# Four modulation chunks of layer 1 formed during the attention of layer 0 instead of during the dense SwiGLU

## Chip, cores and metric

One NeuronCore of a Trainium2 chip runs the whole program. The metric is the device time of one launch in microseconds (us), as the median of three runs. A further launch is recorded instruction by instruction by the hardware profiler; the rows below come from that one.

## What is computed

The reference is a trunk of two layers over 256 latent tokens and 256 context tokens of width 1024. Each layer modulates its input, mixes tokens (a gated linear recurrence, windowed attention and differential attention), and then mixes channels: a dense SwiGLU in layer 0, top-2 of 8 SwiGLU experts in layer 1. The part that matters here is the modulation of each layer:

```python
mod_l = jnp.split((silu_c @ ada_w[layer] + ada_b[layer])[:, None, :], 6, axis=-1)
mod_c = jnp.split(silu_cc @ ada_w[layer] + ada_b[layer], 6, axis=-1)
u_lat = h_lat * (1.0 + mod_l[1]) + mod_l[0]
...
h_lat = layer_norm(DEEPNORM_ALPHA * h_lat + mod_l[2] * m_lat, ln_g[layer, 0], ln_b[layer, 0])
u_lat = h_lat * (1.0 + mod_l[4]) + mod_l[3]
```

`ada_w[layer]` has 1024 rows and 6 x 1024 columns, all in f32: 24 MB a layer. The product has only two rows, one for the latent tokens and one for the context tokens. Of layer 1, the chunks 0 and 1 are wanted when layer 0 is over, chunk 2 after the token mixing of layer 1, chunks 3 and 4 ahead of its experts and chunk 5 after them.

## The kernel before

A scheduler orders each engine's instructions from the program text; tile pools with few buffers decide who waits for whom.

**A modulation group.** `ada(l, g, rowp)` forms two of a layer's six chunks and returns eight closures, called steps here. A step (`step`, L248 to L259) loads 128 rows by 2048 columns of `ada_w` (1 MB) into a tile `raw` by SP's queue and multiplies them by the two conditioning columns, with four matmuls of 512 columns. Each of the four writes two rows of the one PSUM bank `A`, at partition 0, 32, 64 or 96. All eight steps of a group add into that bank. The last step of a group also copies the four pairs of rows out (`row`, L292, two copies on ACT and two on DVE) and transposes them to columns (L295, sixteen 32x32 transposes on PE, in PSUM tiles `T`). `raw` has two buffers, and they also hold the weights of `w_in`, `w_out` and of the SwiGLU's first two products.

**Where the steps are called.** `self.todo` is a list of closures and `fill(n)` calls the next n of them. In the attention, `streams` alternates between a differential head part and a windowed head part for the four token blocks and calls `fill(1)` in every second round; what is left over is called by `fill(99)` when the rounds are done. In layer 0 the list holds the groups (0, 1) and (0, 2): 16 steps. In the dense SwiGLU, `ffn` runs over 11 slices of 256 hidden columns; a slice has 96 matmuls of the two products with W1 and W3 (PSUM tiles `acc` and `S`) and 48 of the product with W2 (PSUM tiles `T`), all 128x512 from its second slice on, and between the two calls `fill(2)`. There the list holds the groups (1, 0) and (1, 1), another 16 steps, with the `mods` of the first group between them.

**After the attention** comes `project`: it loads `w_out` into the `raw` buffers (L780, L783), splits each f32 weight into two parts (`whi` by a cast on ACT, L126; `wlo` by a subtraction on DVE, L127) and multiplies by three matmuls (L107 to L109), as all big products here do. At the end of the attention POOL's queue loads `ctx` and `x` into `hc` and `hl` (L1294, L1295), 1 MB each.

Of the kernel before, what the change touches and what calls it, by code (L numbers as in the profile page):

```python
# [76 lines left out]
class Trunk:  # L77
# [249 lines left out]
    def streams(self, a, b):  # L327

        rest, live, tails, n = [list(a), list(b)], [None, None], [], 0
        while any(live) or any(rest) or tails:  # L330
            tails = [g for g in tails if next(g, self) is not self]
            for j in range(2):
                if j == 1 and n < 6:
                    continue
                if live[j] is None and rest[j]:
                    live[j] = rest[j].pop(0)
                if live[j] and next(live[j]) == "tail":
                    tails.append(live[j])
                    live[j] = None
            n += 1  # L340
            if n % 2 == 0:
                self.fill(1)

    def fill(self, n):
# [898 lines left out]
    def run(self):  # L1243
        tc, nc, i = self.tc, self.nc, self.i
        self.banks = {"acc": 2, "S": 3, "T": 2, "A": 1}
        self.cat = consts(0)[1]
        self.todo, self.cols = [], {}
        all4, lat = [0, 1, 2, 3], [2, 3]
        with ExitStack() as es:
            pool = lambda name, bufs, **kw: es.enter_context(tc.tile_pool(name=name, bufs=bufs, **kw))  # L1250
            self.cp = pool("cp", 1)
            self.stp = pool("stp", 4)
            self.rawp = pool("rawp", 2)
            self.wp = pool("wp", 5)
            pool("edge", 1, side="right").tile([P, 24], F32, name="edge")
            mx = ExitStack()
            right = lambda name, bufs, **kw: mx.enter_context(tc.tile_pool(name=name, bufs=bufs, side="right", **kw))
            self.ps = mx.enter_context(tc.tile_pool(name="ps", bufs=8, space=PSUM))
            self.utp = right("utp", 8)
            self.bdp = right("bd", 1)  # L1260
            rw = right("rw", 1)

            with tc.tile_pool(name="adaw", bufs=6) as adaw, tc.tile_pool(name="u32", bufs=2) as u32p, tc.tile_pool(name="tmp", bufs=1) as self.tmp:
                self.setup()
                into = self.pairs("uh"), self.pairs("ul")
                x = [self.tmp.tile([P, 2, D], F32, name=name) for name in ("xc", "xl")]
                first = self.ada_first(rw, adaw)
                for h in range(2):
                    for k in range(KD):
                        next(first)  # L1270
                        if h:
                            next(products)
                    G, B = self.mods(0, 0, None, slice(4 * h, 4 * h + 4))
                    if h == 0:
                        for n, name in enumerate(("ctx", "x")):
                            nc.sync.dma_start(out=x[n], in_=i[name].rearrange("o (b p) d -> p (o b) d", p=P))
                    uh, ul = self.make_u(lambda tb: x[tb // 2][:, tb % 2], G, B, all4, u32p, into, (2 * h, 2 * h + 1))
                    if h == 0:
                        held = self.copied.ins
                        products = self.lru_products(0, uh, ul, False)  # L1280
                        next(products)
                with tc.issue_after(held):
                    self.params(self.tmp.tile([P, 2048], F32, name="scratch"))
                    bd = self.gate_weights(0)
            self.todo = self.ada(0, 1, rw) + self.ada(0, 2, rw)
            mh, ml = self.mixer(0, uh, ul, all4, bd, products)
            self.dumpm(mh, ml, 0)
            bd = self.gate_weights(1)
            hl = pool("hl", 1).tile([P, 2, D], F32, name="hl")
            with tc.tile_pool(name="hc", bufs=1) as hcp:  # L1290
                hc = hcp.tile([P, 2, D], F32, name="hc")
                h = lambda tb: hc[:, tb] if tb < 2 else hl[:, tb - 2]
                with tc.tile_pool(name="raw2", bufs=2) as raw2, tc.tile_pool(name="ga", bufs=1) as gp, tc.tile_pool(name="res", bufs=1) as self.resp:
                    nc.gpsimd.dma_start(out=hc, in_=i["ctx"].rearrange("o (b p) d -> p (o b) d", p=P))  # L1294
                    nc.gpsimd.dma_start(out=hl, in_=i["x"].rearrange("o (b p) d -> p (o b) d", p=P))  # L1295
                    gate = self.gate(0, 2, [0, 1], gp)
                    G, B = self.mods(0, 3, (0, 0))
                    self.project(0, mh, ml, all4, gate, h, lambda tb: self.norm(h(tb)), raw2)
                self.dumph("ln0", h, all4)
                with tc.tile_pool(name="acc", bufs=1) as accp, tc.tile_pool(name="raw2", bufs=1) as raw2, tc.tile_pool(name="wp2", bufs=3) as wp2, \  # L1300
                        tc.tile_pool(name="fg", bufs=4) as fg:
                    with tc.tile_pool(name="u32", bufs=2) as u32p:
                        uh, ul = self.make_u(h, G, B, [2, 3, 0, 1], u32p)
                    with tc.tile_pool(name="lg", bufs=1) as lgp:
                        self.base(0, 0, h, all4, lgp)
                    with tc.tile_pool(name="ga", bufs=1) as gp, tc.tile_pool(name="res", bufs=1) as self.resp:
                        m1 = []
                        self.todo = self.ada(1, 0, rw) + [lambda: m1.extend(self.mods(1, 0, (0, 1)))]
                        self.todo += self.ada(1, 1, rw)
                        self.ffn(uh, ul, h, (accp, raw2, wp2, fg), lambda: self.gate(0, 5, [0, 1], gp), lambda s: self.fill(2))  # L1310
                        self.fill(99)

                self.dumph("ln1", h, all4)
                G, B = m1
                with tc.tile_pool(name="u32", bufs=2) as u32p:
                    uh, ul = self.make_u(h, G, B, all4, u32p)
            m2 = {}

            def prepare():
                g1 = right("g1", 1)  # L1320
                self.todo.append(lambda: m2.update(gate=self.gate(1, 2, [0], g1)))
                self.todo.append(lambda: m2.update(cols=self.mods(1, 3, (1, 0))))
                self.todo.append(lambda: m2.update(G=self.rows(m2["cols"][0][:, 0], g1, "modg")))
                self.todo.append(lambda: m2.update(B=self.rows(m2["cols"][1][:, 0], g1, "modb")))

            self.todo = self.ada(1, 2, rw)
            h = lambda tb: hl[:, tb - 2]
            with tc.tile_pool(name="lg", bufs=1) as lgp:
                self.base(0, 1, h, lat, lgp)
            self.moe_consts(pool("rc", 1))  # L1330
            mh, ml = self.mixer(1, uh, ul, lat, bd, self.lru_products(1, uh, ul, True), prepare)
            self.dumpm(mh, ml, 1)
            self.RB, self.wn = 7, 0
            self.rawb = pool("rawb", self.RB)
            ro = pool("ro", 1)
            gate2 = self.gate(1, 5, [0], ro)[0]
            with ExitStack() as ms:
                rs = ExitStack()
                rp = rs.enter_context(tc.tile_pool(name="rp", bufs=1))
                u = rp.tile([P, 2, D], F32, name="u")  # L1340
                with tc.tile_pool(name="res", bufs=1) as self.resp:
                    self.project(1, mh, ml, lat, m2["gate"], h, lambda tb: self.modulate(h(tb), u[:, tb - 2], m2["G"], m2["B"]))
                    first = [self.wtile(v) for v in self.up_views(NE - 1, *self.CHUNKS[0])]
                self.dumph("ln2", h, lat)
                mx.close()
                self.ps = pool("psm", 8, space=PSUM)
                self.banks = {"h": 4, "T": 2, "Y": 2}
                pl = lambda name, bufs, side: ms.enter_context(tc.tile_pool(name=name, bufs=bufs, side=side))
                fin = self.moe(hl, u, gate2, ro, rs, pl, first)
                self.final(hl, fin)  # L1350
# [41 lines left out]
```

## Time and profile before

| what | value |
|---|---|
| median of 3 runs | 1671.74 us (1671.57 to 1671.98) |
| the profiled execution | 1673.18 us, its span 1671.3 us |
| PE (TensorE matmul) | 1587.6 us busy, 95% |
| DVE, ACT, POOL | 1221.2, 919.8, 160.9 us busy |
| attention of layer 0 | 156.8 to 268.1 us of the span |
| dense SwiGLU | some 320 to 720 us |
| DMA | 364.77 MB, 218 GB/s on average |

PE is the engine that is busy nearly all the time. The profile models the ends of matmuls, so its share says that it is seldom left without work, not that it does as much as it could.

### The profile page before, as it was taken

Reading aid. Unit: us, or ns where it says so; the run is one execution under the profiler, and the core shown is the slowest. Engines: PE = TensorE matmul, PEld = TensorE weight load, DVE = VectorE, ACT = ScalarE, POOL = GpSimd, SP = SyncE. Lnnn points to the kernel's source line nnn. Section 1 sums busy time; section 2 is a strip of 40 time slices with the busy share of each in tenths; the row PEclk is TensorE's granted clock in tenths of the full one; section 3 lists DMA queues with packets and bytes.
Section 4 is the critical chain, followed back from the end, with each engine's and each line's share of the span. In section 5 each row is a group of like instructions: output and inputs, shape, how many; then the busy total and the mean of one; then the engine's idle time right before and its main releaser. Section 6 shows DMA issues by size and latency. Waiting matters only on the chain. (4 is left out here: it accounts for less than half of the span.)

```text
span 1671.3 us, 21565 instructions
## 1 busy us (share of the span) xinstructions
PE 1587.6 (95%) x7977; PEld 1229.7 (74%) x7977; DVE 1221.2 (73%) x1741; ACT 919.8 (55%) x1298; POOL 160.9 (10%) x131
## 2 busy tenths in 40 slices
PE   7999999999999999989899799999999999999995
PEld 3776566787777777777567588787887878878784
DVE  2678675644443345687976998989888898888987
ACT  2466565423222223246665487777776776767773
POOL 0000012250000000260002200101001010010101
PEclk8999999999999999989999799999999999999998
DMA  8313446224542354212348599898998989989890
GB/s 304 121 54 104 152 152 201 101 94 158 170 157 101 126 166 162 76 54 82 113 141 285 177 393 358 322 377 304 352 347 312 344 316 341 356 310 335 325 355 31
DMA packets 164582, 364.77 MB, mean 218 GB/s; under 512 B 8396, under 2 KB 46120, under 8 KB 159352
## 3 DMA queue, kind: packets, MB, share of 16 engines
q1 hardware_dynamic: 159472, 355.56, 60.6%
q0 software_dynamic: 1840, 6.67, 1.2%
q10 hardware_dynamic: 3160, 1.12, 0.3%
q8 instruction: 64, 1.05, 0.3%
q14 instruction: 46, 0.38, 0.1%
HBM read 362.27 MB, written 1.05 MB: 217 GB/s over the span
## 5 line engine op out<-in xcount | busy, mean ns | idle before, releaser
L127 DVE TENSOR_TENSOR wlo<-rawb,whi 128x1024 fp32r<-128x1024 f32 x362 | 436.0, 1249 | 34.5 <-ACT whi L126 30.6
L126 ACT CAST whi<-rawb 128x1024 fp32r<-128x1024 f32 x362 | 364.3, 1051 | 57.0 <-PE ps_h L109 33.6
L127 DVE TENSOR_TENSOR wlo<-raw,whi 128x1024 fp32r<-128x1024 f32 x214 | 269.2, 1279 | 100.1 <-ACT whi L126 98.7
L126 ACT CAST whi<-raw 128x1024 fp32r<-128x1024 f32 x214 | 218.7, 1051 | 183.8 <-DMA raw<-in_ffn_w_dram 85.6
L108 PE MATMUL ps_h<-wlo,th 128*128 128x512 f32 (+1 forms) x672 | 257.6, 383 | 14.2 <-DVE wlo L127 13.3
L107 PE MATMUL ps_h<-whi,th 128*128 128x512 f32 (+1 forms) x672 | 253.7, 378 | 0.2 <-ACT th L131 0.2
L109 PE MATMUL ps_h<-whi,tl 128*128 128x512 f32 (+1 forms) x672 | 251.8, 375 | 0.0
L108 PEld LDWEIGHTS ps_h<-wlo,th 128*128 128x128 f32 x672 | 127.3, 189 | 51.2 <-DVE wlo L127 30.6
L107 PEld LDWEIGHTS ps_h<-whi,th 128*128 128x128 f32 x672 | 127.5, 190 | 23.0 <-ACT th L131 0.5
L109 PEld LDWEIGHTS ps_h<-whi,tl 128*128 128x128 f32 x672 | 127.4, 190 | 20.6 <-DVE tl L132 0.2
L108 PE MATMUL ps_Y<-wlo,gTh 128*128 128x512 f32 x308 | 122.4, 397 | 0.4
L109 PE MATMUL ps_Y<-whi,gTl 128*128 128x512 f32 x308 | 120.2, 390 | 0.0
L1132 POOL TENSOR_TENSOR hl<-hl,sct 128x512 f32<-128x512 f32 x26 | 45.0, 1759 | 679.5 <-DVE sct L1131 559.5
L107 PE MATMUL ps_Y<-whi,gTh 128*128 128x512 f32 x308 | 108.4, 390 | 0.0
L107 PE MATMUL ps_acc<-uh,whi 128*128 128x512 f32 (+1 forms) x256 | 92.4, 367 | 2.6 <-ACT whi L126 2.3
L108 PE MATMUL ps_acc<-ul,whi 128*128 128x512 f32 (+1 forms) x256 | 94.1, 368 | 0.1
L109 PE MATMUL ps_acc<-uh,wlo 128*128 128x512 f32 (+1 forms) x256 | 92.1, 361 | 0.0
L108 PE MATMUL ps_S<-ul,whi 128*128 128x512 f32 (+1 forms) x240 | 85.7, 357 | 0.0
L107 PE MATMUL ps_S<-uh,whi 128*128 128x512 f32 (+1 forms) x240 | 85.6, 357 | 0.0
L109 PE MATMUL ps_S<-uh,wlo 128*128 128x512 f32 (+1 forms) x240 | 84.9, 355 | 0.0
L107 PE MATMUL ps_acc<-whi,uh 128*128 128x512 f32 (+1 forms) x176 | 71.0, 403 | 0.0
L108 PE MATMUL ps_acc<-wlo,uh 128*128 128x512 f32 (+1 forms) x176 | 69.1, 392 | 0.2 <-DVE wlo L127 0.2
(352 smaller groups left out, 2830.3 us busy)
## 6 DMA issues: line engine op xcount, KB each, us to landing
rawb<-in_moe_w_dram SPq DMA_DIRECT2D x181, 1024.0 KB, 6.7
raw<-in_moe_w_dram SPq DMA_DIRECT2D x50, 1024.0 KB, 6.5
raw<-in_ada_w_dram SPq DMA_DIRECT2D x40, 1024.0 KB, 4.9
raw<-in_ffn_w_dram SPq DMA_DIRECT2D x33, 1024.0 KB, 7.2
raw<-in_w_in_dram SPq DMA_DIRECT2D x16, 1024.0 KB, 5.6
aw<-in_ada_w_dram SPq DMA_DIRECT2D x16, 512.0 KB, 7.0
raw<-in_w_out_dram SPq DMA_DIRECT2D x16, 512.0 KB, 5.6
lg<-in_ln_g_dram POOLq DMA_DIRECT2D x4, 512.0 KB, 4.0
```

The costliest lines, as they stand in the source:

```text
L107: mm(out, lhsT=ah, rhs=bh, start=start, stop=False)
L108: mm(out, lhsT=ah, rhs=bl, start=False, stop=False)
L109: mm(out, lhsT=al, rhs=bh, start=False, stop=stop)
L126: nc.scalar.copy(out=hi, in_=v)
L127: self.last = nc.vector.tensor_tensor(out=lo, in0=v, in1=hi, op=ALU.subtract)
L1132: (nc.vector if quick and nn else nc.gpsimd).tensor_tensor(out=hl[:, b, cs], in0=hl[:, b, cs], in1=t, op=ALU.add)
```

## The change

`streams` calls `fill(1)` after every `self.every` rounds. For layer 0 that number is 1, and its list is extended by the groups (1, 0) and (1, 1) to 32 steps; for layer 1 it is 2 as before. The list of the dense SwiGLU keeps only the `mods` closure. Only four places differ:

```diff
-            if n % 2 == 0:
+            if n % self.every == 0:
                 self.fill(1)
...
-            self.todo = self.ada(0, 1, rw) + self.ada(0, 2, rw)
+            self.todo, self.every = sum((self.ada(l, g, rw) for l, g in ((0, 1), (0, 2), (1, 0), (1, 1))), []), 1
...
-                        self.todo = self.ada(1, 0, rw) + [lambda: m1.extend(self.mods(1, 0, (0, 1)))]
-                        self.todo += self.ada(1, 1, rw)
+                        self.todo = [lambda: m1.extend(self.mods(1, 0, (0, 1)))]
...
-            self.todo = self.ada(1, 2, rw)
+            self.todo, self.every = self.ada(1, 2, rw), 2
```

What the scheduler makes of it shows in the order of PE's instructions. Early in the attention of layer 0, in the program before (`ps_A` is the bank of a modulation group, L255 the matmuls of a step, L656 and L598 to L602 scores, L568 transposes of softmax weights, L673 and L621 products with the values):

```order
L255 MATMUL ps_A<-raw,sc 2x512
L673 MATMUL ps_acc<-pT,dV 64x128 x4
L568 MATMUL ps_T<-cst,p 128x128 x4
L255 MATMUL ps_A<-raw,sc 2x512 x3
L656 MATMUL ps_S<-kdT,qT 128x512
L598 MATMUL ps_S<-kT,qT 128x512
L599 MATMUL ps_S<-kT,qT 128x512
L602 MATMUL ps_S<-maskr,eyer 128x128
L656 MATMUL ps_S<-kdT,qT 128x512
L255 MATMUL ps_A<-raw,sc 2x512
```

At the same place in the changed program:

```order
L255 MATMUL ps_A<-raw,sc 2x512 x4
L673 MATMUL ps_acc<-pT,dV 64x128 x4
L568 MATMUL ps_T<-cst,p 128x128 x4
L656 MATMUL ps_S<-kdT,qT 128x512
L598 MATMUL ps_S<-kT,qT 128x512
L599 MATMUL ps_S<-kT,qT 128x512
L602 MATMUL ps_S<-maskr,eyer 128x128
L255 MATMUL ps_A<-raw,sc 2x512 x4
```

Before, the four matmuls of a step mostly stand as one and three with other work between them; now most steps stand whole. Up to the product with `w_out`, the 16 steps of before stand in 29 pieces on PE, and the 32 steps of now in 38 pieces, the last of which holds three steps.

At the end of the attention of layer 0 on PE, before (L636 and L701 are transposes of results; L107 is the first product with `w_out`):

```order
L255 MATMUL ps_A<-raw,sc 2x512 x3
L568 MATMUL ps_T<-cst,p 128x128 x2
L621 MATMUL ps_acc<-pT,V 64x128
L701 MATMUL ps_T<-cst,mix_647 128x128 x2
L621 MATMUL ps_acc<-pT,V 64x128 x3
L568 MATMUL ps_T<-cst,p 128x128 x4
L621 MATMUL ps_acc<-pT,V 64x128
L568 MATMUL ps_T<-cst,p 128x128
L621 MATMUL ps_acc<-pT,V 64x128 x3
L568 MATMUL ps_T<-cst,p 128x128 x3
L107 MATMUL ps_acc<-whi,mh 128x512
```

And in the changed program (L295 are the transposes that end a group):

```order
L255 MATMUL ps_A<-raw,sc 2x512 x4
L568 MATMUL ps_T<-cst,p 128x128 x4
L621 MATMUL ps_acc<-pT,V 64x128 x4
L568 MATMUL ps_T<-cst,p 128x128 x2
L255 MATMUL ps_A<-raw,sc 2x512 x4
L568 MATMUL ps_T<-cst,p 128x128 x2
L621 MATMUL ps_acc<-pT,V 64x128
L636 MATMUL ps_T<-cst,ra 128x128 x4
L621 MATMUL ps_acc<-pT,V 64x128 x3
L255 MATMUL ps_A<-raw,sc 2x512 x12
L295 MATMUL ps_T<-cst,row 128x32 x12
L107 MATMUL ps_acc<-whi,mh 128x512 x2
```

Of the five last steps two stand between pieces of the attention, and the other three stand one behind the other, after all attention work and ahead of the first product with `w_out`.

SP's queue, which issues the loads, from the steps to the first slices of the SwiGLU. First before:

```order
L253 DMA raw<-in_ada_w_dram 128x2048 x16
L780 DMA raw<-in_w_out_dram 128x2x512 x2
L783 DMA raw<-in_w_out_dram 64x4x512 x2
L780 DMA raw<-in_w_out_dram 128x2x512 x2
L783 DMA raw<-in_w_out_dram 64x4x512 x2
L116 DMA raw<-in_ffn_w_dram 128x8x256 x3
```

Then in the changed program:

```order
L253 DMA raw<-in_ada_w_dram 128x2048 x32
L780 DMA raw<-in_w_out_dram 128x2x512 x2
L783 DMA raw<-in_w_out_dram 64x4x512 x2
L780 DMA raw<-in_w_out_dram 128x2x512 x2
L783 DMA raw<-in_w_out_dram 64x4x512 x2
L116 DMA raw<-in_ffn_w_dram 128x8x256 x3
```

The load of a `w_out` tile stands behind 32 step loads instead of 16, in the same two buffers.

## Rows read from the trace of the kernel before

**Rows 1.** The page: busy time of each engine over the span

```profile
PE 1587.6 (95%) x7977; PEld 1229.7 (74%) x7977; DVE 1221.2 (73%) x1741; ACT 919.8 (55%) x1298; POOL 160.9 (10%) x131
```

**Rows 2.** Windows: attention of layer 0, eight SwiGLU slices, the experts

```profile
core 0: us, PE busy (x) PEld busy (x) DVE busy (x) ACT busy (x) POOL busy (x), PEclk, DMA share, GB/s
156.80:268.10 111.30, 109.01 (x730) 62.22 (x728) 74.80 (x216) 70.13 (x198) 9.95 (x13) 1.00 0.46 152
...
371.20:676.30 305.10, 302.27 (x1401) 234.75 (x1401) 136.62 (x183) 79.64 (x95) 0.53 (x1) 1.00 0.44 145
...
940.00:1671.00 731.00, 699.40 (x3266) 568.33 (x3266) 649.33 (x650) 517.96 (x582) 47.02 (x28) 0.99 0.89 321
```

**Rows 3.** Groups on PE, 371.2 to 676.3 us: busy, mean ns, idle before, releasers

```profile
L107 PE MATMUL ps_T<-whi,gh 128*128 128x512 f32 x144 | 57.8, 401 | 0.9 <-DVE acc L901 0.4
...
L255 PE MATMUL ps_A<-raw,sc 128*2 128x512 f32 x128 | 15.4, 592 | 0.0
L295 PE MATMUL ps_T<-cst,row 32*128 32x32 f32 x32 | 3.4, 225 | 2.0 <-DVE row L292 1.1 <-ACT row L292 0.9
L307 PE MATMUL ps_T<-cst,adac 128*128 128x128 f32 x16 | 2.3, 277 | 0.0
```

**Rows 4.** Windows of PE alone: one slice, and a stretch without steps

```profile
515.78:549.07 33.29, 33.18 (x149) 1.00 0.27 95
664.27:692.65 28.38, 28.38 (x126) 1.00 0.25 82
```

**Rows 5.** Groups on PE, 156.8 to 268.1 us, the attention of layer 0

```profile
L255 PE MATMUL ps_A<-raw,sc 128*2 128x512 f32 x128 | 29.8, 592 | 0.2 <-DMA raw<-in_ada_w_dram 0.2
...
L295 PE MATMUL ps_T<-cst,row 32*128 32x32 f32 x16 | 1.3, 227 | 0.0
```

**Rows 6.** Timeline of PE, attention of layer 0: start us, us, instruction

```profile
157.38 1.04 PE L255 MATMUL ps_A<-raw,sc 128*2 128x512 f32 x8
158.35 0.50 PE L656 MATMUL ps_S<-kdT,qT 128*128 128x512 f32 x1
158.79 1.02 PE L255 MATMUL ps_A<-raw,sc 128*2 128x512 f32 x2
159.74 0.44 PE L530 MATMUL ps_T<-cst,st 128*128 128x128 f32 x2
...
245.94 0.63 PE L568 MATMUL ps_T<-cst,p 128*128 128x128 f32 x4 [0.33 <-DVE p L669]
...
263.77 0.43 PE L621 MATMUL ps_acc<-pT,V 128*64 128x128 f32 x2 [0.56 <-DVE pT L572]
...
265.89 0.50 PE L107 MATMUL ps_acc<-whi,mh 128*128 128x512 f32 x1 [0.36 <-ACT whi L126]
```

**Rows 7.** DMA issues, 157 to 260 us: count, KB each, median us to landing

```profile
raw<-in_ada_w_dram SPq DMA_DIRECT2D x14, 1024.0 KB, 4.9
raw<-in_w_out_dram SPq DMA_DIRECT2D x2, 512.0 KB, 4.3
```

**Rows 8.** DMA issues, 250 to 300 us, the start of the projection

```profile
hc<-in_ctx_dram POOLq DMA_DIRECT2D x1, 1024.0 KB, 10.3
hl<-in_x_dram POOLq DMA_DIRECT2D x1, 1024.0 KB, 14.5
```

**Rows 9.** Timeline of POOL, the issue of those two loads

```profile
268.35 0.92 POOL L1294 DMA_DIRECT2D hc<-in_ctx_dram  x1 [9.16 <-PE ps_T L636]
```

**Rows 10.** Windows ahead of the SwiGLU: PE's busy time and its granted clock

```profile
316.00:318.00 2.00, 0.65 (x4) 0.40 (x4) 1.50 (x2) 1.74 (x3) 1.26 (x1) 1.00 1.04 366
318.00:320.00 2.00, 0.35 (x3) 0.12 (x2) 2.00 (x5) 0.14 (x1) 0.00 (x0) 0.90 1.06 392
320.00:322.00 2.00, 2.00 (x8) 1.52 (x9) 1.74 (x5) 2.00 (x3) 0.55 (x1) 0.50 1.04 380
...
326.00:328.00 2.00, 2.00 (x17) 2.00 (x16) 2.00 (x4) 1.77 (x4) 0.00 (x0) 0.89 0.00 0
```

**Rows 11.** The page: issues of the expert weights, whole span

```profile
rawb<-in_moe_w_dram SPq DMA_DIRECT2D x181, 1024.0 KB, 6.7
```

## The prediction

> **What bounds the kernel now.** I read the page first: PE is busy 95% of the span [rows 1], so the question is whether a step that moves costs PE more or less where it goes. Next come the windows of the two stages. In the attention of layer 0 PE is busy 109.0 of 111.3 us, and in the stretch of the dense SwiGLU from the first to the last step 302.3 of 305.1 us [rows 2]; both run at the full granted clock (1.00, the 2.4 GHz level). Neither stage has idle time in which a step could be had for nothing: the attention's many small matmuls fill PE as fully as the SwiGLU's large ones. DMA is no bound in either (share 0.46 and 0.44) [rows 2]. So the change moves work from one full stage to another, and the sum is one of PE time at both ends, plus what the transfers add.
>
> The groups of PE then show the surprise. The 16 steps (128 records; an f32 matmul leaves two) take 15.4 us in the SwiGLU [rows 3] and 29.8 us in the attention [rows 5]. The timeline says why: a whole step (x8, four matmuls) lets the next instruction start 0.97 us later, and a single matmul of a step (x2) holds PE for 0.95 us just the same [rows 6]. The four write to four groups of columns and run side by side; a piece costs about 0.96 us whether it holds one of them or four. Before, the attention's 16 steps stand in 29 pieces, which makes 29 x 0.96 = 28 us.
>
> **What the SwiGLU gets back.** The stretch of 305.1 us holds 1401 PE instructions [rows 2], of which 128, 32 and 16 are steps, row transposes and gate transposes [rows 3]; the other 1225 are 128x512 matmuls. Without steps these ran at 0.227 us each (28.38 us for the 125 that the window holds whole), and in the slice that holds only one step, which lies ahead of the window, at 0.231 us (33.29 us for 144) [rows 4]; the difference is T banks that DVE has not yet emptied (0.4 us in all is named for the first of each three) [rows 3]. So 1225 matmuls take 278.1 to 283.0 us, the gate transposes stay (2.3), and 19.8 to 24.7 us come free. Counted directly the steps' 15.4, the transposes' 3.4 and the 2.0 us that PE waits for the row copies make 20.8 [rows 3]. With no step between, the product with W2 follows the other products at once and DVE has the time of two steps (1.9 us) less for its silu work first, so I don't take the upper end: **22.5 us less**.
>
> **What the attention pays.**
> Pieces: 38 instead of 29, the last of which holds three steps, so 40 against 29. 11 x 0.96 = **10.6 us more** (11.3 by the 1.03 us of a record). The doubling of the steps costs only a third more, since most now stand whole.
> Transposes: 32 more at a group's end. 16 take 1.3 us here [rows 5], 32 take 3.4 in the SwiGLU [rows 3]: **3.0** (2.6 to 3.4).
> Row copies: at the end of a group PE waits for ACT and DVE if its transposes stand right behind the last step. That happened once in the SwiGLU and cost 2.0 us [rows 3]; in the attention of before other work stood between and no such wait is named [rows 5]. In the new order two of four ends have nothing between, the first group's and the last one's: 0 to 4.0, taken as **3.0**, the last in full and half of the first.
> The last three steps: they stand together behind all attention work. A load is issued when the step before the last has freed its buffer, and lands 4.9 us later [rows 7]. Attention work takes (109.0 - 29.8) / (730 - 128) = 0.13 us a record [rows 2, 5], so the 14 records between the 28th and 29th step, and the 14 between the 29th and 30th, take 1.8 us each. Count from the end of the 28th step: the 29th ends at 2.8; the 30th is wanted at 4.6, lands at 4.9 and ends at 5.9; the 31st, issued at 2.8, lands at 7.7 and ends at 8.7; the 32nd, issued at 5.9, lands at 10.8 and ends at 11.8. PE waits 0.3 + 1.8 + 2.1 = 4.2 us. But POOL's 2 MB of `hc` and `hl` start when the last transposes L636 of the attention are through [rows 9], which now is ahead of those three steps, and in such a stretch a transfer of 1 MB took 10.3 and 14.5 us [rows 8]. If the 32nd step's load takes 10.3, the waits make 9.6. I take **6.5**, between the ends, since a load on SP's queue landed in 4.9 and only one of the three meets both of POOL's.
> The rule that speaks against the change stands here: the Trainium skill (Trainium Kernel Development and Optimization, Key Constraints) says that transfers issued from SP, ACT and POOL run on the same 16 DMA engines and interleave. By it the 9.6 would hold and the sum be 3.1 us higher; the 10.3 and 14.5 us agree with it.
> `w_out`: its first tile is issued when the 31st step is over, lands 4.3 us later [rows 7] at 13.0, and is cast while the last group's transposes still run; the second is issued at 11.8. Behind the group's end stand 16 gate transposes and the first half of the products as cover: **0.5** (0 to 2).
> Hidden waits: the attention's end now has 0.33 + 0.56 + 0.36 = 1.2 us of waits [rows 6], which then lie ahead of the three steps whose own waits cover the lateness: **-1.2**.
> The clock: ahead of the SwiGLU PE was busy 1.0 of 4 us, the granted clock fell to 0.50 (the 1.2 GHz level) and stayed there for some 6 us, in which 3 us of work are lost [rows 10]. The waits of the last steps make a stretch like it: PE would be idle for 7.5 us ahead of the 32nd step if its load is late, and busy 1.9 of the 4 us up to 11.8 if not. Part of the slow time would pass in the copies' wait: 0 to 3.0, taken as **2.0**.
> The Trainium skill's page TensorE: Matmul & The Clock Gate (HAM oscillation) describes the same fall for kernels whose loads leave gaps between bursts of matmuls. By it the 3.0 would be paid in full and the sum be 1.0 us higher; rows 10 agree.
>
> The `mods` closure stays in the SwiGLU on DVE, which is busy 137 of 305 us there [rows 2], and costs nothing; if that cover were gone, it would be below 1 us. In the attention the copies and small additions of two more groups go to ACT (70 of 111 us) and DVE (75 of 111) [rows 2], which have room as long as PE is the slower.
>
> Sum: 10.6 + 3.0 + 3.0 + 6.5 + 0.5 - 1.2 + 2.0 = 24.4 against 22.5: **1.9 us longer**. The profiled execution took 1673.18 us, 1.44 more than the median of the runs, so 1675.1 by its own time, and 1673.6 for the median.
>
> **The rivals.**
> *The end of the attention is cheap.* The three loads land in 4.9 us, POOL's transfers start too late to meet them, and without the long wait the clock holds: 2.3 and 2.0 less, and 1.5 less for copies that find ACT and DVE idle. That is 18.6 against 22.5, 3.9 shorter: 1667.8. For it speaks that the loads of the attention landed in 4.9 [rows 7]; against it that the tail's loads are the first to meet POOL's.
> *The end of the attention is dear.* POOL's loads are ahead of the last step's: 3.1 more, the clock's full 3.0, the first group's wait in full: 5.1 more, 1678.7. It decides from the point at which the 32nd load lands later than some 8 us after its issue.
> *The loads become the bound of the whole attention.* It would last some 128 us, 4.0 for each of 32 steps. A buffer comes round every 8.0 us; 1.0 goes to the matmuls, so a load may take 7.0 before every step waits. Expert loads landed in 6.7 at a DMA share of 0.89 [rows 2, 11], and here the rate goes from 152 to some 260 GB/s (16 MB more in 128 us). At 6.7 only steps with less than 3 us between them wait, some 0.5 to 1 us for 10 to 15 of the 32: 10 more, 1683.6. Against it: 0.2 us of such wait before [rows 5].
> That the change doesn't do what it says is excluded by the order of instructions: the steps do stand in the attention.
>
> **How the numbers follow.** From 1671.74, 0.2% is 3.3 us, about what a measurement of this kernel can tell from no change. The sum as it stands has 0.45, with 1669 to 1675 as its own range; the cheap end 0.21; the dear end 0.22; the loads as the bound 0.12. So faster by over 0.2% has 0.21, within it 0.45, slower 0.34. The range of 8 in 10 goes from 1666.5, just past the cheap end, to 1681, past the dear end, and leaves the last rival out.
>
> **What would show it right or wrong.** In the changed profile the stretch of the SwiGLU that now takes 305.1 us should take some 282.6; steps in the attention should be busy some 39 us; the three last steps should wait on `raw` 4 to 10 us; and the attention with its end should be some 24 us longer. That stretch at 288 or more, steps that wait on `raw` all through the attention, or an end of attention without waits would each make the prediction wrong.

## The result and the profile after

The changed kernel takes 1685.65 us (median of four runs, 1681.75 to 1688.66) against 1671.65 us before in the same runs: 14.0 us longer, ratio 1.0076 with a 95% interval of 1.0064 to 1.0089. The forecast was 1673.6 and its range ended at 1681.0.

The profiled execution took 1688.66 us, its span 1686.9, 15.6 more than before. PE's busy time in it, from the page, which answers to [rows 1]:

```profile
PE 1589.7 (94%) x7977; PEld 1233.7 (73%) x7977; DVE 1232.0 (73%) x1741; ACT 920.7 (55%) x1298; POOL 161.6 (10%) x131
```

PE works 2 us more and the span is 15.6 us longer, so most of what came on top is time in which PE stood still or for which the busy time tells nothing. Where it lies, two windows tell: the stage "attention" from the first modulation step to the last product with `w_out`, and the stage "SwiGLU" from the first product behind that to the last product with W2. In the trace of before (columns as in [rows 2]):

```profile
157.38:314.82 157.44, 155.15 (x951) 100.45 (x951) 98.49 (x264) 85.14 (x217) 24.66 (x26) 1.00 0.45 148
320.53:718.80 398.27, 392.75 (x1877) 311.37 (x1876) 195.26 (x249) 108.54 (x134) 40.71 (x24) 0.99 0.40 133
```

and in the changed kernel's:

```profile
155.73:352.60 196.87, 181.94 (x1112) 110.45 (x1112) 105.43 (x288) 88.09 (x221) 25.19 (x27) 0.92 0.62 203
358.30:733.75 375.45, 369.97 (x1716) 306.29 (x1716) 198.90 (x225) 106.24 (x130) 41.24 (x23) 1.00 0.29 96
```

The SwiGLU gives back 22.8 us, as forecast (22.5). The attention pays 39.4 instead of 24.4, and its mean granted clock is 0.92 instead of 1.00. The two make 16.6 us and the spans differ by 15.6, because in this execution the stage also began 1.65 us earlier and what follows the SwiGLU took 0.6 us longer.

For all that follows the attention stage is split in three, from windows of 2 us. **Idle** is the window less PE's busy time. **Slow clock** is the busy time times one minus the granted clock, what the work would have saved at the 2.4 GHz level. The **rest** is work at the full clock. All in us, from one profiled execution each, which can lie some us from the kernel's median (e3's took 1677.76 us with a median of 1681.74):

| kernel | attention | idle | slow clock | rest | SwiGLU |
|---|---|---|---|---|---|
| before | 157.4 | 2.3 | 0.0 | 155.1 | 398.3 |
| changed | 196.9 | 14.9 | 11.4 | 170.5 | 375.5 |
| changed, second profile (e12) | 198.2 | 16.3 | 11.5 | 170.4 | 374.4 |
| three groups in the attention (e3) | 173.7 | 9.0 | 3.4 | 161.4 | 388.6 |
| the same, transposes later (e8) | 176.6 | 8.4 | 7.9 | 160.3 | 386.8 |
| 28 steps in the attention (e10) | 178.0 | 6.9 | 5.0 | 166.1 | 383.4 |
| changed, `hc` and `hl` loaded later (e13) | 194.7 | 11.1 | 13.5 | 170.0 | 374.3 |
| changed, PE kept busy at group ends (e4) | 194.8 | 9.7 | 5.9 | 179.2 | 373.7 |
| changed, PE kept busy at the end (e11) | 194.9 | 9.9 | 6.7 | 178.4 | 374.7 |
| before, steps early (e5) | 162.3 | 10.0 | 5.1 | 147.2 | 400.0 |
| before, steps early, transposes later (e6) | 160.1 | 9.1 | 2.8 | 148.2 | 400.0 |
| before, 4 steps instead of 16 (e9) | 144.3 | 9.5 | 1.5 | 133.3 | 400.0 |
| before, more loads (e7) | 186.4 | 23.6 | 10.3 | 152.5 | 401.2 |

So of the 39.4 us, 15.4 are work, 12.6 idle time and 11.4 slow clock. Where the last two arise shows in PE's timeline. At the first group's end:

```profile
181.66 1.04 PE L255 MATMUL ps_A<-raw,sc 128*2 128x512 f32 x8
183.48 0.94 PE L295 MATMUL ps_T<-cst,row 32*128 32x32 f32 x8 [0.79 <-ACT row L292]
184.87 0.80 PE L598 MATMUL ps_S<-kT,qT 128*128 128x512 f32 x1 [0.44 <-ACT p L661]
185.60 0.63 PE L295 MATMUL ps_T<-cst,row 32*128 32x32 f32 x4
...
187.55 1.87 PE L255 MATMUL ps_A<-raw,sc 128*2 128x512 f32 x2
```

The group's transposes stand right behind its last step and wait 0.79 us for a row copy; 0.44 us for the softmax follow; and from there a piece of a step takes 1.87 us instead of 1.02. The windows of the same place, and of the end of the attention, show the granted clock that does it (columns as in [rows 2]):

```profile
182.00:184.00 2.00, 1.10 (x13) 0.33 (x5) 2.00 (x7) 1.15 (x2) 0.00 (x0) 1.00 1.07 385
184.00:186.00 2.00, 1.56 (x9) 1.01 (x9) 1.77 (x6) 0.78 (x2) 0.00 (x0) 0.67 0.88 315
186.00:188.00 2.00, 2.00 (x10) 1.18 (x9) 1.19 (x7) 0.00 (x0) 0.17 (x1) 0.50 0.41 172
188.00:190.00 2.00, 2.00 (x5) 0.65 (x4) 0.00 (x0) 0.00 (x0) 0.35 (x1) 0.50 0.00 0
...
288.00:290.00 2.00, 0.30 (x4) 0.00 (x0) 0.89 (x3) 0.71 (x2) 1.62 (x2) 1.00 1.08 373
...
298.00:300.00 2.00, 0.60 (x4) 0.50 (x4) 1.12 (x5) 0.00 (x0) 0.00 (x0) 0.50 0.96 351
```

PE's timeline at the end, from the 30th step on:

```profile
287.26 1.04 PE L255 MATMUL ps_A<-raw,sc 128*2 128x512 f32 x8
290.23 1.68 PE L255 MATMUL ps_A<-raw,sc 128*2 128x512 f32 x8 [1.93 <-DMA raw<-in_ada_w_dram]
293.68 1.89 PE L255 MATMUL ps_A<-raw,sc 128*2 128x512 f32 x8 [1.76 <-DMA raw<-in_ada_w_dram]
296.31 1.23 PE L295 MATMUL ps_T<-cst,row 32*128 32x32 f32 x8 [0.75 <-ACT row L292]
298.08 0.60 PE L295 MATMUL ps_T<-cst,row 32*128 32x32 f32 x4 [0.54 <-DVE row L292]
301.62 1.22 PE L107 MATMUL ps_acc<-whi,mh 128*128 128x512 f32 x2 [2.94 <-ACT whi L126]
...
306.09 1.97 PE L307 MATMUL ps_T<-cst,adac 128*128 128x128 f32 x8 [1.21 <-ACT gate L308]
```

Up to 287.26 us the stage has 5.8 us of idle time and 5.0 of slow clock; from there on, 9.1 and 6.5. Steps wait for their loads only here: in the attention ahead it is 0.6 us in all, as the groups of PE there show, which answer to [rows 5]:

```profile
L255 PE MATMUL ps_A<-raw,sc 128*2 128x512 f32 x236 | 40.8, 605 | 0.6 <-DMA raw<-in_ada_w_dram 0.6
...
L295 PE MATMUL ps_T<-cst,row 32*128 32x32 f32 x48 | 5.2, 236 | 1.7 <-ACT row L292 0.8 <-DVE row L292 0.7
```

and their loads land as fast as before, while `w_out` lands late (DMA issues from 255 us on, which answer to [rows 7, 8]):

```profile
raw<-in_ada_w_dram SPq DMA_DIRECT2D x8, 1024.0 KB, 4.9
raw<-in_w_out_dram SPq DMA_DIRECT2D x8, 512.0 KB, 13.4
...
hc<-in_ctx_dram POOLq DMA_DIRECT2D x1, 1024.0 KB, 9.4
hl<-in_x_dram POOLq DMA_DIRECT2D x1, 1024.0 KB, 12.5
```

### The profile page after: what moved, and what is told of

Same layout as the page of the kernel before. It is cut to its first block, busy times and chain, and to the rows that moved or that the text cites. A ratio compares the mean times of both kernels' runs of the same rounds, so it can differ in the third digit from the quotient of the medians.

```text
span 1686.9 us, 21584 instructions
## 1 busy us (share of the span) xinstructions
PE 1589.7 (94%) x7977; PEld 1233.7 (73%) x7977; DVE 1232.0 (73%) x1741; ACT 920.7 (55%) x1298; POOL 161.6 (10%) x131
## 5 line engine op out<-in xcount | busy, mean ns | idle before, releaser
L127 DVE TENSOR_TENSOR wlo<-raw,whi 128x1024 fp32r<-128x1024 f32 x214 | 273.8, 1301 | 124.4 <-ACT whi L126 122.9
L107 PE MATMUL ps_h<-whi,th 128*128 128x512 f32 (+1 forms) x672 | 253.7, 378 | 0.2 <-ACT th L131 0.2
L107 PEld LDWEIGHTS ps_h<-whi,th 128*128 128x128 f32 x672 | 127.4, 190 | 23.1 <-ACT th L131 0.5
L107 PE MATMUL ps_Y<-whi,gTh 128*128 128x512 f32 x308 | 108.3, 390 | 0.0
L107 PE MATMUL ps_acc<-uh,whi 128*128 128x512 f32 (+1 forms) x256 | 91.6, 364 | 2.6 <-ACT whi L126 2.3
L107 PE MATMUL ps_S<-uh,whi 128*128 128x512 f32 (+1 forms) x240 | 85.5, 357 | 0.2 <-DVE u L380 0.2
L901 DVE TENSOR_TENSOR acc<-ps_T,acc 128x512 f32<-128x512 f32 x72 | 48.8, 688 | 35.9 <-PE ps_T L109 35.9
L582 DVE TENSOR_REDUCE mx<-ps_S 128x1 f32<-128x512 f32 (+1 forms) x80 | 54.3, 687 | 24.4 <-PE ps_S L656 13.2
```

The source lines that it names most:

```text
L107: mm(out, lhsT=ah, rhs=bh, start=start, stop=False)
L127: self.last = nc.vector.tensor_tensor(out=lo, in0=v, in1=hi, op=ALU.subtract)
L582: self.nc.vector.reduce_max(mx[:, h0:h0 + per], b.rearrange("p (r k) -> p r k", r=per), axis=AX.X)
L901: nc.vector.tensor_tensor(out=a, in0=b, in1=a, op=ALU.add)
```

## The experiments

The theory to begin with: the 15 us that the forecast missed are lost where PE waits and the clock then falls, at the ends of the groups in the middle of the attention and at its end. The rivals: the loads through two buffers bound the whole attention; or it is only the pieces, more work than the sum had.

### Steps kept whole (e1, e2)

```diff
-            for j in range(4):
-                nc.tensor.matmul(A[32 * j:32 * j + 2, :], ...)
+            with self.tc.tile_critical():
+                for j in range(4):
+                    nc.tensor.matmul(A[32 * j:32 * j + 2, :], ...)
```

> The kernel before, with the four matmuls of each modulation step kept together on PE, so that its 16 steps in the attention of layer 0 stand in 16 pieces instead of 29. If a piece costs 0.96 us whether it holds one matmul or four, 13 pieces less make the attention 12.5 us shorter: 1659. If the group ends are what costs (a step's transposes right behind it, PE waiting for the row copies and the clock falling to 0.5), up to 5 us of it are given back: 1664. If the four matmuls cost what they cost in any order, or the keeping together costs as much elsewhere: 1671 to 1673.

> The changed kernel with the steps kept together in the same way: 32 pieces for 40. The last four steps instead of three now stand behind all attention work. If only the pieces count: 7.7 us shorter, 1678. If the three last steps, the late w_out and the clock at the end are the larger cost, one more step there gives 3 to 4 us back: 1681 to 1682. If the loads bound the attention, fewer pieces gain nothing: 1685 or more, and the steps wait on raw all through the attention.

Measured: 1817.05 us (ratio 1.0861, 1.0845 to 1.0876) and 1807.47 (1.0807, 1.0787 to 1.0827). Both missed by far and tell nothing of the pieces. The waits of SP's queue in e1, from 157 to 320 us (what waits, for what: us in total, times, longest):

```profile
SPq L253 <- PEq L254: 154.4, 14, 31.4
```

And those of PE there:

```profile
PE ps_A L256 <- DMA raw<-in_ada_w_dram: 22.6, 5, 5.7
```

A critical section holds back the load of a step until PE's sequencer has come to the section, so no load runs ahead any more: 145 us for the program's 40 steps, 3.6 each on average. What a piece costs was then read from other kernels.

### Three groups, and 28 steps (e3, e10)

In e3 the last group stays in the SwiGLU; in e10 its last four steps do.

```diff
-  ... for l, g in ((0, 1), (0, 2), (1, 0), (1, 1))), []), 1
+  ... for l, g in ((0, 1), (0, 2), (1, 0))), []), 1            # e3
+  ... ((0, 1), (0, 2), (1, 0), (1, 1))), []), 1                # e10
+            self.todo, left = self.todo[:28], self.todo[28:]   # e10
...
+                        self.todo += self.ada(1, 1, rw)        # e3
+                        self.todo += left                      # e10
```

> The changed kernel with three groups in the attention of layer 0 (24 steps, 32 pieces) and the fourth left in the dense SwiGLU: no step stands behind the attention work and w_out is loaded as early as before. The SwiGLU gives back half of the 23 us, 11.5; the attention pays 3 pieces (2.9) and 16 transposes (1.5). If that were all: 1664.6. If the group ends in the middle of the attention cost what the changed kernel's trace shows (the clock at 0.50 and 0.66 behind the first two, and 3 us of waits), 8 us come on top: 1672 to 1673. If the loads bound the attention, 24 steps at 4.0 us are 96 of 111 us, no bound any more: also 1665.

> The changed kernel with 28 steps in the attention and the last four of the fourth group in the SwiGLU; the rest of the attention's order is that of the changed kernel. If the end of the attention (three steps behind all its work, w_out late, half clock) is where the largest part of the loss is, 8 us of waits, 6.5 us of slow clock and 4 us of steps and transposes go, and the SwiGLU pays 5 to 6: 1674 to 1678. If the loss lies all through the attention: 1683 to 1686.

Measured: e3 1681.74 us (1.0053, 1.0034 to 1.0072; runs from 1675.16 to 1684.85), e10 1677.1 (1.0023, 1.0013 to 1.0033). For e10 the theory of the end held to the term in the attention: against the changed kernel's profile 8.0 us less idle time, 6.5 less slow clock and 4.4 less work. The SwiGLU pays 7.9, where 5 to 6 were expected. With no step behind the attention's work, products with `w_out` (L107) begin between its last pieces, and neither the steps nor `whi` nor the gate are waited for (PE's timeline of e10):

```profile
281.04 1.04 PE L255 MATMUL ps_A<-raw,sc 128*2 128x512 f32 x8
282.01 0.83 PE L568 MATMUL ps_T<-cst,p 128*128 128x128 f32 x4
282.97 0.43 PE L621 MATMUL ps_acc<-pT,V 128*64 128x128 f32 x2
283.34 0.50 PE L107 MATMUL ps_acc<-whi,mh 128*128 128x512 f32 x1
```

e3 missed: its attention is 16.3 us longer than before with only 8 steps more. Its work grew by 6.3 us, and 6.7 of idle time and 3.4 of slow clock came with it, though no step stands at its end. Of its waits, 3.7 us are for the softmax (1.6 before), 2.3 for DVE's `res` in the products with `w_out` (none before; e5 below shows where that comes from) and 1.5 for row copies.

### PE kept busy (e4, e11)

Matmuls that nobody reads, 128x256, fill PE's waits: in e4 8 at each group end and 16 ahead of each of the last two steps; in e11 60 at the end alone.

```diff
+    def warm(self, b, n):
+        for _ in range(n):
+            self.nc.tensor.matmul(b[:, 0:256], lhsT=self.eyer, rhs=..., start=True, stop=True)
...
+            if (l, g) == (1, 1) and k >= 6:
+                self.warm(self.bank("T"), 14)     # in step, e11
...
+        if l == 1 and c in (2, 3):
+            self.warm(pt, 8)                      # in ada_cols, ahead of the transposes, e11
```

> The changed kernel with idle PE time filled: 8 matmuls that nobody reads, 128x256, about 0.12 us each, ahead of the transposes at each of the four group ends in layer 0, and 16 ahead of each of the last two steps. If the slow clock is a large part of the 15 us that the forecast missed, the granted clock stays at 1.0 behind the group ends and through the last steps, and the time falls by 6 to 10 us less some 2 us that the added matmuls cost where PE wasn't idle: 1677 to 1682. If the clock costs little and it is waits, loads or pieces: 1685 to 1690.

> The changed kernel with its end alone kept busy: 60 matmuls that nobody reads, 128x256, ahead of each of the last two steps and between the last group's transposes, 7 to 8 us where the changed kernel's trace shows 9 us of idle PE. The attention ahead of them is unchanged. If the slow clock there costs the 6.5 us that the trace shows: the granted clock stays at 1.0 through the end, 1679 to 1681. If the clock costs nothing (PE waits there anyway for loads and casts): 1685 to 1688.

Measured: e4 1686.18 us (1.0084, 1.0070 to 1.0097), e11 1686.75 (1.0093, 1.0079 to 1.0107). Neither gained. In e4 idle time and slow clock fell by 10.7 us together, and the rest, which holds the added matmuls themselves, grew by 8.7: what they filled and what they took nearly cancel. (The scheduler also put the attention into another order there, from the last steps of the first group on, so the two sums are not of the matmuls alone.) In e11 the last step still waited 3.35 us for its load, behind the added work, and the clock fell there as before; the slow clock from there on is 5.0 instead of 6.5. So filling waits did not pay here; that the clock at the end costs 6.5 us is not shown by these two but by e10, where the waits themselves are gone.

e11 shows something else. Up to the last five steps its PE order is that of the changed kernel but for one pair of matmuls behind this place, and at the first group's end PE reaches the same instructions at the same times, within 0.02 us, with the same waits:

```profile
181.68 1.04 PE L257 MATMUL ps_A<-raw,sc 128*2 128x512 f32 x8
183.50 0.94 PE L304 MATMUL ps_T<-cst,row 32*128 32x32 f32 x8 [0.79 <-ACT row L298]
184.89 0.51 PE L607 MATMUL ps_S<-kT,qT 128*128 128x512 f32 x1 [0.44 <-ACT p L670]
...
186.53 1.02 PE L257 MATMUL ps_A<-raw,sc 128*2 128x512 f32 x2
```

Yet the piece of a step takes 1.02 us: here the clock did not fall. The same two gaps cost 3.3 us of slow clock in one execution and nothing in another.

### Steps early, and transposes later (e5, e6, e8)

e5 changes only the kernel before: its own 16 steps, one after every round.

```diff
-            self.todo = self.ada(0, 1, rw) + self.ada(0, 2, rw)
+            self.todo, self.every = self.ada(0, 1, rw) + self.ada(0, 2, rw), 1
```

e6 and e8 take the transposes out of a group's last step and put them behind four further steps or rounds (the row copies stay); e6 is e5 with that, e8 is e3 with that:

```diff
+            a, b, no = self.ada(0, 1, rw, True), self.ada(0, 2, rw, True), lambda: None
+            self.todo, self.every = a[:8] + b[:4] + a[8:] + b[4:8] + [no] * 4 + b[8:], 1
```

> The kernel before with its own two groups in the attention of layer 0, one step after every round instead of every second one: its 16 steps stand in 19 pieces instead of 29, early in the attention, and the transposes that end the two groups stand right behind their last steps, in the same order on PE as the first two groups of the changed kernel. Nothing is moved out of the SwiGLU. If only the pieces count (0.96 us each): 9.6 us shorter, 1662. If the group ends cost what they cost in the changed kernel (row copies waited for, the clock at 0.50 behind the first): 6 to 8 us of that are given back, 1668 to 1670. If loads at this pace are the bound: 1671 or more, with waits on raw throughout.

> The run before this one (16 steps early in the attention, 20 pieces), with the transposes of each group's end put behind four further steps or rounds instead of right behind the last step; the row copies stay where they are. If the group ends are what costs: PE no longer waits for the copies, the granted clock stays at 1.0 through the attention, 1662 to 1664. If they cost nothing: the same as the run before this one, or 1 us more for the one piece more.

> Three groups in the attention and the fourth in the SwiGLU, as in the run with three groups (1681.7), with the transposes of each group put behind four further steps; 33 pieces for 32. If the group ends cost 6 to 8 us: 1674 to 1676, with the granted clock at 1.0. If not: 1681 to 1683.

Measured: e5 1677.83 us (1.0032, 1.0020 to 1.0044), e6 1675.01 (1.0015, 1.0003 to 1.0026), e8 1679.86 (1.0039, 1.0026 to 1.0052). e5 is the most telling run of the study: 10 pieces fewer, and the kernel is slower. Its time would fit the loads as the bound, but the steps' waits for loads are 0.7 us. The work did shrink. PE's steps there take 19.7 us instead of 29.8 [rows 5]:

```profile
L255 PE MATMUL ps_A<-raw,sc 128*2 128x512 f32 x128 | 19.7, 592 | 0.7 <-DMA raw<-in_ada_w_dram 0.7
```

and the rest of the stage fell by 7.9 us, most of the 9.6 that 10 pieces make. But 7.7 us of idle time and 5.1 of slow clock took their place. PE's longest waits in e5's stage:

```profile
PE ps_acc L107 <- DVE res L800: 2.4, 1, 2.4
PE ps_T L568 <- DVE p L669: 1.9, 2, 1.1
PE ps_acc L621 <- DVE rb L638: 1.2, 1, 1.2
PE ps_S L598 <- ACT p L661: 1.1, 2, 0.6
```

The waits for the softmax are 4.2 us in all, against 1.6 before, and 0.8 are for a row copy. The longest wait stands behind the attention: a product with `w_out` waits until DVE has emptied its bank into `res`. `res` has two buffers, and POOL, which adds them to `hl` and so frees them, waits 14.6 us for the load of `hl` (POOL's timeline of e5):

```profile
285.74 1.25 POOL L801 TENSOR_TENSOR hl<-hl,res 128x512 f32<-128x512 f32 x1 [14.62 <-DMA hl<-in_x_dram]
```

That wait also stands in e3, e6, e8, e9 and e10 (1.1 to 2.6 us), and in e5 1.7 us of slow clock follow it. Up to the first product with `w_out` e5 takes 107.6 us against 108.5 before, so the 9.6 us of pieces bought 0.9 there. The theory that follows: **in this stage the steps are cover.** The steps, split and spread through the rounds, fill moments in which PE would wait for the chain of the softmax through DVE and ACT. In e5 this accounts for a part of the idle time only; e9 tests it.

The transposes put later gained 2.8 us (e6 against e5) and 1.9 (e8 against e3), where 6 to 8 were expected, and the intervals overlap; e6's own time, 1662 to 1664, was missed by 11 us. The waits for row copies go (in e6 none is named), but the clock falls elsewhere: 7.9 us of it in e8's profile.

### Fewer steps (e9)

```diff
-        return [lambda k=k: step(k) for k in range(KD)]
+        return [lambda k=k: step(k) for k in (range(KD) if (l, g) not in ((0, 1), (0, 2)) else (0, KD - 1))]
```

> The kernel before with 12 of its 16 steps in the attention of layer 0 left out (the first and the last of each group stay, so the modulation is not the reference's): 6 pieces instead of 29, some 22 us less work for PE. If PE's work sets the length of the attention, as the prediction took it: 1650. If the steps mostly fill time in which PE would wait for the softmax on DVE and ACT, and keep the clock up (in the run with early steps 9.4 us less of pieces came back as 7.7 us of idle time and 5.1 of slow clock): 1664 to 1672.

Its total (1998.08 us) compares with nothing, since with another modulation the experts take more instructions (PE executes 9285 instead of 7977), so the stage is read. Its rest is 21.9 us shorter, as 23 pieces at 0.96 us make (22.1); the stage is 13.1 us shorter, between the two expectations, nearer the second. 7.2 us came back as idle time and 1.5 as slow clock. The waits for the softmax are 7.0 us, 5.4 more than before, and 1.6 are for `res`. So the theory holds in part: some three fifths of the work taken out did shorten the stage, and a quarter came back as waits for the softmax. PE's timeline where a step's pieces stood before shows the chain that they covered:

```profile
163.99 0.50 PE L656 MATMUL ps_S<-kdT,qT 128*128 128x512 f32 x1 [0.92 <-ACT p L661]
164.85 0.63 PE L568 MATMUL ps_T<-cst,p 128*128 128x128 f32 x4 [0.36 <-DVE nb L657]
165.93 0.77 PE L598 MATMUL ps_S<-kT,qT 128*128 128x512 f32 x1 [0.46 <-ACT p L661]
```

### The loads (e7, e13)

e7 adds 16 MB of loads to the attention of before. e13 takes `hc` and `hl` off POOL's queue:

```diff
+            if self.junk and n <= 32:                                             # e7, in streams
+                self.nc.gpsimd.dma_start(out=self.junk[0], in_=...)               # 512 KB
...
-                    nc.gpsimd.dma_start(out=hc, in_=...)                          # e13
-                    nc.gpsimd.dma_start(out=hl, in_=...)
...
+            for t, name in zip(load, ("ctx", "x")) if n == 0 else ():             # in project,
+                nc.sync.dma_start(out=t, in_=...)                                 # behind w_out's first tiles
```

> The kernel before with 16 MB of further loads in the attention of layer 0, 32 loads of 512 KB on POOL's queue that nobody reads, so that the DMA traffic there is that of the changed kernel and the work of PE is not. If the loads are the bound of the attention: its steps wait on raw, 5 to 10 us longer, 1677 to 1682. If not: 1672 to 1674.

> The changed kernel with the loads of hc and hl taken off POOL's queue and issued on SP's behind the first two w_out tiles, so that neither the last steps' loads nor the first w_out tile meet them; PE's order stays. If these 2 MB are what makes the end of the attention long (raw waits of 3.7 us, whi 2.9 and gate 1.2, with the first w_out load landing some 8 us after its issue): the waits shrink by 3 to 5 us and the slow clock with them by 1 to 3: 1679 to 1682. If the end is long because the last steps and w_out share two buffers, one load after the other: 1684 to 1686, with the same waits.

Measured: e7 1703.41 us (1.0181, 1.0164 to 1.0198), e13 1681.93 (1.0051, 1.0034 to 1.0068). e7 is longer than any theory had, for a reason of its own. The waits of PE in it, from 156 to 290 us:

```profile
PE ps_T L703 <- POOL mix L698: 11.8, 2, 11.5
PE ps_A L255 <- DMA raw<-in_ada_w_dram: 3.1, 2, 3.0
```

and those of POOL:

```profile
POOL junk L342 <- DMA junk<-in_ada_w_dram: 99.3, 22, 9.0
```

All added loads write one tile, so POOL waits for each of them, and its work on `mix` comes late. In the products with `w_out` PE waits another 5.0 us for `wlo`. The steps' loads took 6.5 us instead of 4.9, and steps waited 3.1 us for them in all. So the run doesn't tell what traffic alone costs; it does tell that steps waited only 3.1 us at 223 GB/s (156.27 to 285.6 us), in a stage that other waits had stretched.

e13 does tell the two causes at the end apart. Its PE timeline, from the 31st step on:

```profile
293.50 1.19 PE L255 MATMUL ps_A<-raw,sc 128*2 128x512 f32 x8 [2.02 <-DMA raw<-in_ada_w_dram]
296.45 1.89 PE L255 MATMUL ps_A<-raw,sc 128*2 128x512 f32 x8 [1.76 <-DMA raw<-in_ada_w_dram]
...
301.39 1.22 PE L107 MATMUL ps_acc<-whi,mh 128*128 128x512 f32 x2
...
304.97 1.97 PE L307 MATMUL ps_T<-cst,adac 128*128 128x128 f32 x8 [0.32 <-ACT gate L308]
```

The waits on `raw` stay (3.8 us against 3.7): they are the chain of loads through two buffers, each issued when the step before the last is over. The wait for `whi` (2.94) is gone and that for the gate is 0.9 shorter: it was the first tile of `w_out` that POOL's loads held up. By medians this is worth 3.7 us, with runs that overlap (1677.46 to 1685.29 against 1681.75 to 1688.66). In the profiled run the clock fell at the third group's end too, as in e12, so that its slow clock is the longest of all.

The Trainium skill (Trainium Kernel Development and Optimization, Key Constraints) has transfers from different engines' queues interleave on the same 16 DMA engines. For `w_out` the runs agree: its first tile reached ACT's cast 8.6 us behind its issue with POOL's loads beside it and at most 4.9 without. For the last steps they don't show it, as their waits were the same with POOL's loads and without.

### The changed kernel again (e12)

> The changed kernel unchanged, for a second profile. If the falls of the clock are what makes its times scatter by 7 us: the two profiles differ in idle time and slow clock by what their times differ, and agree in the rest of PE's time to 1 us. If the work itself varies: the rest differs too.

Measured: 1690.36 us, one run. The rest agrees with the first profile to 0.1 us (170.4 and 170.5), and so does the idle time up to the 30th step (5.8 both times); at the end it is 1.4 us longer. The slow clock agrees only in its sum: 6.6 us in the middle, where the clock fell at the third group's end too, and 4.9 at the end, against 5.0 and 6.5. The 1.7 us between the two runs are this 1.4, a stage that begins 1.5 us later and a SwiGLU that is 1.1 us shorter. So between these two profiles the work stayed the same, and the idle time at the end and the place of the slow clock changed. Nothing here was faster than the kernel before; nearest were e6 and e10, 0.15% and 0.23% above it.

## Why the prediction was wrong

**The SwiGLU: right.** 22.5 us were forecast, 22.8 came (23.9 in e12). Split like the attention, 21.4 of them are work; the other 1.4 are less slow clock, which the forecast did not have. The idle time stayed 5.5: the 2.0 us of row copies [rows 3] are gone, and a product with W2 now waits once, 1.9 us, for DVE's `acc`. That DVE would have less time was the forecast's reason not to take the upper end.

**Pieces and transposes: right, and the rest 1.8 us short.** 10.6 and 3.0 make 13.6; the rest grew by 15.4. The price of 0.96 us a piece is shown by e9 (23 pieces, 21.9 us) and by e5 (the same 16 steps in 10 pieces fewer, busy 10.1 us less). Counted in the traces from each PE instruction's start to the next one's, at the granted clock, the steps grew by 10.8 us and the transposes by 3.2; the other 1.4 us lie with scores and transposes in another order, and why is not shown.

**The waits: 3.8 us short in sum, and two causes changed places.** 8.8 were forecast, 12.6 came.
- Row copies: 3.0 forecast, 2.8 named in the trace (1.5 for ACT's, 1.3 for DVE's). The sum is near by luck: three ends waited and not two, 0.8 us at the first, 0.7 at the third and 1.3 at the last, for which 2.0 were taken.
- The last three steps: 6.5 forecast between 4.2 and 9.6, 3.7 measured. The lower end, the chain through two buffers, was the right count; the reason for going above it, POOL's loads, e13 refutes.
- `w_out`: "0.5 (0 to 2)" was the mis-sized term: 2.9 us for `whi`, and 1.2 for the gate behind it. The first tile's loads did not land in the 4.3 us of [rows 7]: issued from 291.95 us on, they reached ACT's cast at 300.5. POOL's loads, priced against the steps, belonged here (e13).
- "Hidden waits: -1.2" did not come; the waits on the softmax (`p`, `nb`, `pT`) grew from 1.6 us to 3.0.

**The clock: the step that failed.** "0 to 3.0, taken as 2.0", and only ahead of the 32nd step. It was 11.4 us: 6.5 at the end, where the low level lasted from 290 to 311 us while wait followed upon wait (in e10, without these waits, the clock stays at 1.00 there), and 5.0 in the middle, behind the first two group ends, where the forecast had none. It had read [rows 10] as a matter of long gaps. In the middle the clock of the profiled run fell behind a 0.79 and a 0.44 us wait close together, and the second time behind one of 0.62 us for the softmax. The Trainium skill (TensorE: Matmul & The Clock Gate, A second HAM failure mode: psum-queue depth-cycling) describes a PE that idles only briefly, but often, between groups of matmuls, and whose clock then swings. The trace agrees that short waits can be followed by a fall (granted 0.67, then 0.50, behind the first two); what PE waited for here was a row copy and the softmax, and not the cycling through PSUM banks of the page's kernel. The prediction drew only on the part about loads.

**What stood behind it.** The prediction took the attention for a stage that PE's work bounds, since PE was busy 109.0 of 111.3 us [rows 2]. e5 and e9 show it otherwise: 9.6 us fewer of pieces made it no shorter, 22.1 fewer made it 13.1 shorter. Before, with the steps split and spread, PE waited 2.3 us in all and the clock stayed at 1.00.

So the loss of 16.6 us in the two stages falls into three parts. Putting one step after every round instead of every second costs 4.9 in the attention, with nothing moved (e5). Twelve further steps then cost 15.7 there (1.3 each) and free 14.9 in the SwiGLU (e10): near nothing. The last four steps cost 18.9 (4.7 each) and free 7.9. The medians say the same: e5 and e10 are each 4.9 us over the kernel before, the changed kernel 14.0. So two thirds of the loss come with the last four steps, three of which stand behind all attention work, and most of the other third with the early place of the first sixteen.

**The rivals.** "The loads become the bound of the whole attention" gave 1683.6, the nearest time, by a mechanism that did not happen: 0.6 us of waits on `raw` up to 287 us. "The end of the attention is dear" had the right place and too small a price, by the wrong transfer.

What stays open: how the 4.9 us of the early place divide between the softmax, the group ends and the wait for `hl`, since e6 and e8 move the group ends without settling it; why e3, with fewer steps than e10, is slower by its median (1681.74 against 1677.1, with runs that overlap); and what makes the clock fall at a gap in one execution and not in another.

## What to carry to other kernels

A stage in which PE is busy 98% of the time may be one in which movable work partly covers another engine's chain: before moving work into it or out of it, ask what PE would wait for without it, and what it will wait for at the seams. Price the clock at every new wait of PE, not only at long ones, and look behind the moved work for loads that queue in the same buffers. And split a stage into idle time, slow clock and rest: in two profiles of the changed kernel the rest agreed to 0.1 us, while the kernel's time scatters by several.

## What the runs showed of the hardware

- The granted clock can fall to 0.50 behind two waits of 0.79 and 0.44 us, or not, with PE at the same instructions at the same times within 0.02 us up to there (the changed kernel and e11, 3.3 us apart there).
- Four matmuls to four groups of columns cost PE 0.97 us together and 0.95 one alone [rows 6]; taking 23 such pieces out made the rest of a stage 21.9 us shorter.
- A critical section around a step's matmuls held its load back until PE came to it: 3.6 us a step on average (e1).
